# One row of the HGRN stage's table rewritten: gates as steps of their own, masked copies and a vector-matrix product placed elsewhere

## The chip, the core and the metric

The kernel runs on one core of a Trainium2 chip, in one launch. A core has five engines that run side by side, each through its own queue in order: PE (matmul; its weight loads are shown apart as PEld), DVE (elementwise), ACT (activation functions, copies), POOL (elementwise, no access to PSUM) and SP, which here only issues DMAs. Engines wait for each other through semaphores. The metric is device time in microseconds, over several runs; a profile is one further execution, whose own time and whose span (first to last instruction) are both given.

## The reference, cut to what matters

The program is two decoder blocks on 256 tokens of width 1024. The first has an HGRN2 mixer, a SwiGLU network, an attention layer and a second network; the second block has four small attention mixers and a convolutional network. All is fp32. The change lies in the HGRN2 mixer of the first layer and touches the conditioning vectors computed beside it:

```python
mod = c_act @ mod_w[layer] + mod_b[layer]                 # (1, 1024) @ (1024, 6144)
sh1, sc1, g1, sh2, sc2, g2 = jnp.split(mod, 6, axis=-1)
u = modulate(rms_norm(h, norm_mix[layer]), sh1, sc1)
q, z_f, v, g = jnp.split(u @ w_in, ...)                   # (256, 1024) @ (1024, 4096)
q = jax.nn.silu(q)
sig = jax.nn.sigmoid(z_f)
f = lbf + (1 - lbf) * sig                                 # the gate, per token and key channel
log_f = jnp.log(jnp.maximum(f, 1e-30))
k = (1 - lbf) * (1 - sig)
# per chunk of 64 tokens and head: attn[t, s] = sum_d q[t] * exp(cumsum difference) * k[s]
# o = attn @ v + (q * exp(b)) @ state;  state = exp(b_last) * state + (k * ...) @ v
o = o * lax.rsqrt(mean(o * o) + eps) * o_gain * silu(g)
h = h + g1 * (o @ w_out)
u = modulate(rms_norm(h, norm_ffn[layer]), sh2, sc2)      # into the SwiGLU network
```

## The kernel before, in words

Activations lie transposed in SBUF: 128 channels on the partitions, tokens along the free side; 256 tokens of two heads, a "pair", are one 128x512 tile. There are four pairs (0 to 3). A weight of 512 KB is a "unit". SP loads it into one of 7 raw buffers; ACT casts it to a high part (`w_hi`, line 193), DVE subtracts to get the low part (`w_lo`, line 195), and PE takes three products per tile (lines 258 to 260: high by high, high by low, low by high). `pump` (before each step of the program) issues loads as raw buffers come free and converts units at most two ahead of the one in use.

The HGRN stage begins with the products of f for pairs 0 and 1 and of q for all pairs (`lin_first`, line 809 in the new text, 806 in the old; the last quarter is `lf[3]`, three units). When the last quarter of f is done, `ev_f` takes the sigmoid on ACT and calls `gates_of` at once: for each head two DVE instructions (lines 748 and 749), and one more for the pair (line 750), five in all per pair; then `hg_t`, six short POOL multiplies (line 856) that give the products of f over 2, 4, ... 64 tokens, `dp`.

The rest of the stage is a list of short steps whose order is written by hand in the string `HG_ORDER`. The first letter is the kind, the first digit the pair:

- `f30` is the first half of a product of f for pair 3 (24 matmuls of 256 columns; `f20`, `f21`, `f31` alike), `v0` to `v7` are the eight units of v (12 matmuls of 512 columns), `w..` those of the output gate; `fa`, `fb`, `fc` are the gates of pairs 2 and 3 from their products, in three steps, the last with four ACT instructions and the DVE line 750.
- `s08` to `s00` are the scores of pair 0 at nine distances (PE: levels 8 to 3 are 16 matmuls of 32x32 tiles, line 896; each bank of PSUM, `pb_b`, of which there are three, holds two levels; 2, 1 and 0 are lines 915, 909, 902). Level 8 reads q, the others `qp` = q times f, made by `d0` (DVE line 847).
- `u06` to `u00` follow each level: a POOL multiply of k (lines 867, 873) and a DVE multiply of `qp` (lines 868, 874) by the products of f of that length. The scores of the next level need both.
- `c00`, `c01`, `c02` take a full score bank out of PSUM by masked copies into `cb` (DVE line 926, two per step; the third also copies on DVE and ACT, line 930). Only then is the bank free.
- `t2`, `t3` are `hg_t` for the later pairs; `pv`, `sq`, `st`, `r`, `n`, `m`, `o`, `ol` are output and norm of a pair, and `a0` to `a5` the output product with its residual.
- `y20` to `y27` are the eight units of the vector-matrix product for g1, on DVE: two instructions a step on raw weights into `ga` (line 516 first, then line 518). `y30`.. and `y40`.. (sh2 and sc2) are on PE: eight small matmul records a step (line 524). `q2` sums up, `z2`, `z3`, `z4` put the vectors in place.

Each engine runs its instructions in the order of this string, so what stands late on DVE delays whatever waits for DVE.

Of the kernel before, what the change touches and what calls it, by code (L numbers as in the profile page):

```python
# [11 lines left out]
F32R = mybir.dt.float32r  # L12
# [34 lines left out]
tr5 o0 y46 y47 pv4 tr6 o1 o2 z3 q4 pv5 pv6 tr7 o3 pv7 z4 o4 o5  # L47
"""
HG_ORDER = """
d0 d1 y20 f20 f21 s08 s18 s07 s17 u06 u16 y21 f30 fa2 c00 c10 s06 s16 u05 u15 fb2 y22 f31 s05 s15 c01 c11 u04  # L50
u14 fc2 y23 y30 v0 fa3 s04 s14 u03 u13 fb3 y31 v1 s03 s13 c02 c12 u02 u12 fc3 d2 y32 y24 v2 s28 s27 s02 s12 u01
u11 u26 t2 y33 v3 s01 s11 u00 u10 c20 s26 u25 d3 y34 v4 s00 s10 s38 s37 u36 s25 u24 t3 y35 y25 v5 pv0 sq0 c21
s24 u23 c30 s36 u35 y36 v6 st0 r0 s23 u22 s35 u34 y37 y26 v7 n0 pv1 sq1 c22 s22 u21 c31 s34 u33 z3 w00 st1 r1
s21 u20 s33 u32 y27 y40 w01 n1 s20 c32 s32 u31 y41 w10 wa0 s31 u30 pv2 sq2 wb0 y42 q2 w11 wc0 s30 st2 r2 m0 wa1
y43 w20 o0 wb1 ol0 pv3 sq3 n2 wc1 y44 z2 w21 m1 st3 r3 y45 w30 o1 ol1 wa2 n3 y46 w31 wb2 wc2 m2 y47 a0 wa3 o2
ol2 wb3 a1 wc3 m3 z4 a2 o3 ol3 a3 a4 a5
"""


# [72 lines left out]
def kernel(ctx: ExitStack, tc: tile.TileContext, x, c, mod_w, mod_b, norm_mix, norm_ffn,  # L132
# [19 lines left out]
    def slot(i, dt=F32, w=2048):  # L152
        return big.tile([P, w], dt, name=f"s{i}", tag=f"s{i}", bufs=1)
# [573 lines left out]
    T = {}  # L727
# [8 lines left out]
        T["v"] = [v[:, 0:D], v[:, D:2 * D]]  # L736

    steps.append(Step(start_hgrn))
    qf_evac = []
    def gates_of(sg, j):  # L740
        for m in range(2):
            h = 2 * j + m
            s_ = sg[:, 256 * m:256 * m + 256]
            if j > 1:
                SC.activation(T["f"][:, h], s_, AF.Identity, bias=lb[:, h:h + 1], scale=one_lb[:, h:h + 1])
                SC.activation(T["k"][:, h], s_, AF.Identity, bias=one_lb[:, h:h + 1], scale=cols[:, 24 + h:25 + h])
                continue
            DV.tensor_scalar(T["f"][:, h], s_, one_lb[:, h:h + 1], lb[:, h:h + 1], op0=OP.mult, op1=OP.add)
            DV.tensor_scalar(T["k"][:, h], s_, cols[:, 24 + h:25 + h], one_lb[:, h:h + 1], op0=OP.mult, op1=OP.add)
        DV.tensor_scalar(pair("f", j), pair("f", j), 1e-30, None, op0=OP.max)  # L750

    def pair(n, j):
        return T[n][:, 2 * j:2 * j + 2].rearrange("p k t -> p (k t)")

    def sig_a(t):
        DV.tensor_scalar(t, t, 2.0 ** 60, None, op0=OP.min)

    def sig_b(t):

        SC.activation(t, t, AF.Ln, bias=ones[:, 0:1], scale=1.0)  # L760
        SC.activation(t, t, AF.Exp, scale=-1.0)

    for j in range(2):
        def ev_f(p, j=j):
            sg = small(512, "sig", 2)
            SC.activation(sg, p, AF.Sigmoid)
            gates_of(sg, j)
            hg_t(j)
        qf_evac.append(ev_f)
    for j in range(4):  # L770
        def ev_q(p, j=j):
            SC.activation(T["q"][:, 2 * j:2 * j + 2].rearrange("p k t -> p (k t)"), p, AF.Silu)
        qf_evac.append(ev_q)
# [9 lines left out]
    for j in range(4):  # L783
        def ev_g(p, j=j):
            G[j] = small(512, "sq", 3)
            SC.activation(G[j], p, AF.Exp, scale=-1.0)
            DV.tensor_copy(pair("sg", j), p)
        for n, st in enumerate(lin_A(wa, 3072 + 256 * j, act("u0"), ev_g, acc_bank)):
            items[f"w{j}{n}"] = [st]
        items[f"wa{j}"] = [Step(lambda j=j: sig_a(G[j]))]  # L790
        items[f"wb{j}"] = [Step(lambda j=j: sig_b(G[j]))]
        items[f"wc{j}"] = [Step(lambda j=j: DV.tensor_mul(pair("sg", j), pair("sg", j), G[j]))]
    G = {}
    first = {}

    def lin_first(h, a, u):

        xhi, xlo = ubox["u0"]
        if h == 0 and a == 0:
            for n in range(2):  # L800
                first[n] = acc_bank()
            for w, x_, k in ((u.hi, xhi, 0), (u.hi, xhi, 1), (u.hi, xlo, 0), (u.hi, xlo, 1), (u.lo, xhi, 0), (u.lo, xhi, 1)):
                for n in range(2):
                    for m in range(2):
                        c0 = 256 * n + P * m
                        PE.matmul(first[n][:, 256 * m:256 * m + 256], lhsT=w[:, k, c0:c0 + P], rhs=x_[:, k],
                                  start=m == 0 and k == 0 and w is u.hi and x_ is xhi, stop=False, skip_group_check=True)
# [12 lines left out]
    lf = [[Step(lambda u, h=h, a=a: lin_first(h, a, u), [unit_A(wa, 256 * h, (1024, 0, 512)[a], 2, 512)], 2.6)  # L820
           for a in range(3)] for h in range(4)]
    for h in range(4):
        steps += [Step(lambda h=h: u0_part(h, LOOK if h == 3 else 1))] + [Step(start_w)] * (h == 3) + lf[h][:1]
        if h < 3:
            if h == 0:
                steps += xp[2:4]
            steps += gq[h + 1][:5] + lf[h][1:2] + gq[h + 1][5:] + lf[h][2:]
            if h == 2:
                steps += [Step(start_t)]
        else:  # L830
            steps += lf[h][1:]

    v_steps = []
    for j in range(2):
# [1006 lines left out]
    for i, it in enumerate(mixers):  # L1841
        kind, p = it
# [49 lines left out]
```

## Time and profile before

| | |
|---|---|
| time, median of 3 runs | 1148.94 us (1146.13 to 1149.74) |
| the profiled execution's own time | 1142.66 us |
| its span | 1140.9 us |
| PE busy, share of the span | 1098.1 us, 96% |
| DVE, ACT, POOL busy | 763.4, 573.4, 138.1 us |
| mean granted PE clock | 0.994 |

A busy PE is not PE at its peak, since matmuls overlap; what PE lost is read from its idle time and from the granted clock. The HGRN stage's hand-ordered list runs from about 68 us to about 197 us of the span. In the rows, `s` is one of the big slots (q, k, f, v lie there), `pb_acc` and `pb_b` are PSUM banks.

### The profile page before, as it was taken

What the parts mean: (1) busy time and instruction counts of PE and PEld (TensorE: products, weight loads), DVE (VectorE), ACT (ScalarE), POOL (GpSimd) and SP (SyncE); (2) the same over time, 40 slices, a digit from 0 to 9 for tenths busy, and PEclk for the clock granted to TensorE, in tenths of its full rate; (3) what the DMA queues carried; (4) which work ended last, traced back from release to release, by engine and by line L of the source; (5) the groups of instructions that cost most, each with busy time, mean ns of one, the idle gap of its engine ahead of it and who ended that gap; (6) DMA issues with size and microseconds to landing.
All of it is one profiled execution on the core that took longest, in us unless ns stands there. A gap on an engine that the chain in (4) does not pass through costs nothing.

```text
span 1140.9 us, 23598 instructions
## 1 busy us (share of the span) xinstructions
PE 1098.1 (96%) x9689; PEld 1014.4 (89%) x9689; DVE 763.4 (67%) x1237; ACT 573.4 (50%) x913; POOL 138.1 (12%) x201
## 2 busy tenths in 40 slices
PE   6988999999999999999999999999999999999997
PEld 4885789899999979888999999988888999999997
DVE  3586765787787688885564454667766766666666
ACT  3455464644444566555444444646555544554454
POOL 4044400000000001250000000013312100000000
PEclk9998999999999999999999999999999999999999
DMA  9976777798988777865766556773343656555651
GB/s 276 318 262 205 224 223 239 257 298 305 302 280 298 232 237 234 292 239 170 237 197 209 185 188 169 153 214 112 116 145 94 217 183 191 186 183 185 192 178 56
DMA packets 176125, 241.92 MB, mean 212 GB/s; under 512 B 18713, under 2 KB 142161, under 8 KB 176017
## 3 DMA queue, kind: packets, MB, share of 16 engines
q1 hardware_dynamic: 174928, 239.54, 66.4%
q8 instruction: 76, 1.25, 0.4%
q0 software_dynamic: 912, 0.81, 0.3%
q14 instruction: 33, 0.26, 0.1%
q10 hardware_dynamic: 176, 0.07, 0.0%
HBM read 239.33 MB, written 1.05 MB: 211 GB/s over the span
## 4 chain that ended last, share of the span: by engine, by line
PE 82%; DVE 6%; DMA 4%; ACT 4%; issue 2%; POOL 1%; SPq 0%; DVEq 0%; ACTq 0%; POOLq 0%
PE pb_b L258 14%; PE pb_b L260 14%; PE pb_b L259 14%; PE pb_acc L258 11%; PE pb_acc L260 10%; PE pb_acc L259 10%; DVE w_lo L195 2%; DMA w_raw<-in_a_w_in_dram 2%; ACT w_hi L193 2%; PE pb_b L463 1%; PE pb_b L1216 1%; DMA w_raw<-in_mod_w_dram 1%; DMA w_raw<-in_kv_w_dram 1%; PE pb_gv L524 1%; DVE nt L573 1%
## 5 line engine op out<-in xcount | busy, mean ns | idle before, releaser
L195 DVE TENSOR_TENSOR w_lo<-w_raw,w_hi 128x1024 fp32r<-128x1024 f32 (+1 forms) x335 | 409.3, 1246 | 172.7 <-ACT w_hi L193 172.0
L258 PE MATMUL pb_b<-s,w_hi 128*128 128x256 f32 x1488 | 419.4, 282 | 5.1 <-ACT s L1750 2.9
L260 PE MATMUL pb_b<-s,w_lo 128*128 128x256 f32 x1488 | 416.2, 280 | 1.6 <-DVE w_lo L195 1.5
L259 PE MATMUL pb_b<-s,w_hi 128*128 128x256 f32 x1488 | 417.3, 280 | 0.3
L193 ACT CAST w_hi<-w_raw 128x1024 fp32r<-128x1024 f32 (+1 forms) x336 | 342.1, 1043 | 79.3 <-DMA w_raw<-in_a_w_in_dram 19.2
L258 PEld LDWEIGHTS pb_b<-s,w_hi 128*128 128x128 f32 x1488 | 280.3, 188 | 12.7 <-issue 4.0
L260 PEld LDWEIGHTS pb_b<-s,w_lo 128*128 128x128 f32 x1488 | 280.3, 188 | 2.6 <-DVE w_lo L195 2.6
L259 PEld LDWEIGHTS pb_b<-s,w_hi 128*128 128x128 f32 x1488 | 280.3, 188 | 1.9 <-DVE s L585 0.7
L260 PE MATMUL pb_acc<-s,w_lo 128*128 128x256 f32 x656 | 183.4, 280 | 4.0 <-DVE w_lo L195 4.0
L258 PE MATMUL pb_acc<-s,w_hi 128*128 128x256 f32 x656 | 186.7, 285 | 0.6 <-ACT w_hi L193 0.6
L259 PE MATMUL pb_acc<-s,w_hi 128*128 128x256 f32 x656 | 183.1, 279 | 0.0
L258 PEld LDWEIGHTS pb_acc<-s,w_hi 128*128 128x128 f32 x656 | 123.3, 188 | 5.8 <-issue 3.5
L260 PEld LDWEIGHTS pb_acc<-s,w_lo 128*128 128x128 f32 x656 | 123.3, 188 | 4.8 <-DVE w_lo L195 4.8
L259 PEld LDWEIGHTS pb_acc<-s,w_hi 128*128 128x128 f32 x656 | 123.4, 188 | 0.2
L1209 POOL TENSOR_SCALAR att<-att,sm 128x128 f32<-128x128 f32 (+1 forms) x72 | 46.7, 668 | 619.4 <-DVE sm L1202 337.7
L1063 ACT CAST s<-sig 128x512 fp32r<-128x512 f32 x38 | 23.6, 621 | 115.9 <-DVE sig L1073 115.9
L258 PE MATMUL pb_acc<-w_hi,s 128*128 128x512 f32 x192 | 78.3, 408 | 1.7 <-ACT s L579 1.0
L259 PE MATMUL pb_acc<-w_lo,s 128*128 128x512 f32 x192 | 76.6, 399 | 0.8 <-DVE w_lo L195 0.8
L260 PE MATMUL pb_acc<-w_hi,s 128*128 128x512 f32 x192 | 76.5, 399 | 0.0
L1776 ACT ACTIVATE sig<-att,vb_t,vc_t 128x256 f32<-128x256 f32 x32 | 17.5, 595 | 75.4 <-DVE att L1771 75.4
L1069 ACT ACTIVATE sig<-pb_b 128x512 f32<-128x512 f32 x22 | 13.2, 598 | 77.8 <-PE pb_b L260 77.7
L1786 POOL TENSOR_TENSOR sig<-sig,rstd 128x512 f32<-128x512 f32 x16 | 22.7, 1420 | 237.2 <-ACT sig L1784 237.2
(373 smaller groups left out, 1255.7 us busy)
## 6 DMA issues: line engine op xcount, KB each, us to landing
w_raw<-in_mod_w_dram SPq DMA_DIRECT2D x96, 512.0 KB, 4.9
w_raw<-in_ffn_w_in_dram SPq DMA_DIRECT2D x88, 512.0 KB, 5.2
w_raw<-in_ffn_w_out_dram SPq DMA_DIRECT2D x44, 512.0 KB, 4.8
w_raw<-in_a_w_in_dram SPq DMA_DIRECT2D x32, 512.0 KB, 5.5
w_raw<-in_ffn_w_gate_dram SPq DMA_DIRECT2D x32, 512.0 KB, 3.8
w_raw<-in_ffn_w_up_dram SPq DMA_DIRECT2D x32, 512.0 KB, 5.3
w_raw<-in_ffn_w_down_dram SPq DMA_DIRECT2D x32, 512.0 KB, 3.6
w_raw<-in_kv_mod_w_dram SPq DMA_DIRECT2D x16, 512.0 KB, 5.8
```

The source lines that it names most:

```text
L193: SC.copy(hi, raw)
L195: DV.tensor_sub(lo, raw, hi.bitcast(F32))
L258: PE.matmul(o, lhsT=whi, rhs=xhi, start=start, stop=False, skip_group_check=True)
L259: PE.matmul(o, lhsT=whi, rhs=xlo, start=False, stop=False, skip_group_check=True)
L260: PE.matmul(o, lhsT=wlo, rhs=xhi, start=False, stop=stop, skip_group_check=True)
L463: PE.matmul(st[:, 0:256], lhsT=mean_d, rhs=sq[:, 256 * m:256 * m + 256], start=j == 0 and m == 0, stop=j == n - 1 and m == 1)
L524: PE.matmul(g[32 * j:32 * j + 32, 0:256], lhsT=by, rhs=r, start=start, stop=stop, tile_position=(0, 32 * j))
L1063: SC.copy(hi, hid)
L1069: SC.activation(sg, g, AF.Silu)
L1209: GP.tensor_scalar(t[:, i, cs], t[:, i, cs], r[:, 2 * b + i:2 * b + i + 1], 1.0, op0=OP.mult, op1=OP.mult)
L1776: SC.activation(zm, am, AF.Identity, bias=vcol("conv_b")[:, f:f + 1], scale=vc_t[:, 64 + f:65 + f])
L1786: GP.tensor_mul(zp, zp, rs_pair())
```

## The change

Four things, all in the HGRN stage:

1. The gates of pairs 0 and 1 are no longer computed inside the evacuation of f. `ev_f` keeps the sigmoid, and two new steps, `first_gates(0)` and `first_gates(1)`, stand between the units of `lf[3]`. Since `pump` runs before each step, a conversion of a coming unit falls before each.
2. In `HG_ORDER` the masked copies come directly after the scores and updates of their bank (`c00 c10` before `f30`, `c01 c11` after `u04 u14`, `c20` before `t2`, `c30 c21` before `t3`), and `d2` (`qp` of pair 2) moves from behind `c02 c12 u02 u12 fc3` to before them.
3. The vector-matrix products change places: `y4` (PE) is first, one unit between products, `y2` (DVE) starts at its old fourth part and runs to the end of the pairs' scores, and `y3` (PE) comes last. No unit is added or removed.
4. The split of the outputs (`ohi`, `olo`) lies in slots 3 and 4, which held q and k, instead of in eight tiles of the stage's pool.

```diff
 HG_ORDER = """
-d0 d1 y20 f20 f21 s08 s18 s07 s17 u06 u16 y21 f30 fa2 c00 c10 s06 s16 u05 u15 fb2 y22 f31 s05 s15 c01 c11 u04
+d0 d1 f20 f21 s08 s18 s07 s17 u06 u16 c00 c10 y40 f30 fa2 s06 s16 u05 u15 fb2 y41 f31 s05 s15 u04 u14 c01 c11
...
@@ gates
-    qf_evac = []
+    qf_evac, G = [], {}
...
             SC.activation(sg, p, AF.Sigmoid)
-            gates_of(sg, j)
-            hg_t(j)
+            G["f", j] = sg
         qf_evac.append(ev_f)
+
+    def first_gates(j):
+        gates_of(G["f", j], j)
+        hg_t(j)
+
...
-            steps += lf[h][1:]
+            for j in range(2):
+                steps += [Step(lambda j=j: first_gates(j))] + lf[h][1 + j:2 + j]
...
     def hg_o(p):
         o = T["f"][:, 2 * p:2 * p + 2].rearrange("p k t -> p (k t)")
-        hi, lo = ph(512, "ohi", 4, F32R), ph(512, "olo", 4, F32R)
+        if p == 0:
+            T["ohi"], T["olo"] = slot(3, F32R), slot(4, F32R)
+        hi, lo = (T[n][:, 512 * p:512 * p + 512] for n in ("ohi", "olo"))
```

First place, on DVE at the end of `lf[3]`: the five gate instructions of pair 0, then of pair 1 (`s_257` is f, `s_256` is k, `cols` the lower bounds), and the low parts of the next units.

```order
 L724 TENSOR_SCALAR cols<-cols 128x8
+L195 TENSOR_TENSOR w_lo<-w_raw,w_hi 128x1024
 L748 TENSOR_SCALAR s_257<-sig,cols 128x256
 L749 TENSOR_SCALAR s_256<-sig,cols 128x256
@@ -63,4 +64,5 @@
 L749 TENSOR_SCALAR s_256<-sig,cols 128x256
 L750 TENSOR_SCALAR s_257<-s_257 128x512
+L195 TENSOR_TENSOR w_lo<-w_raw,w_hi 128x1024
 L748 TENSOR_SCALAR s_257<-sig,cols 128x256
 L749 TENSOR_SCALAR s_256<-sig,cols 128x256
```

A low part now stands ahead of the gates of pair 0 and another between the pairs, where all three stood behind both.

Second place, on DVE from the first `qp` to the update of level 5, before: `ga` is the sum of `y2`, `cb` the masked copies' target.

```order
L847 TENSOR_TENSOR qp<-s_254,s_257 128x512 x2
L516 TENSOR_SCALAR ga<-w_raw,ca 128x512 x2
L195 TENSOR_TENSOR w_lo<-w_raw,w_hi 128x1024
L874 TENSOR_TENSOR qp<-qp,s_257 128x256 x2
L518 SCALAR_TENSOR_TENSOR ga<-w_raw,ca,ga 128x512 x2
L195 TENSOR_TENSOR w_lo<-w_raw,w_hi 128x1024
L756 TENSOR_SCALAR s_256<-s_256 128x512
L926 COPY_PREDICATED cb<-pairm,pb_b 128x128 x4
L874 TENSOR_TENSOR qp<-qp,dp 128x128x2 x2
```

And the same stretch now (lines are shifted by 4):

```order
L851 TENSOR_TENSOR qp<-s_254,s_257 128x512 x2
L195 TENSOR_TENSOR w_lo<-w_raw,w_hi 128x1024
L878 TENSOR_TENSOR qp<-qp,s_257 128x256 x2
L930 COPY_PREDICATED cb<-pairm,pb_b 128x128 x4
L195 TENSOR_TENSOR w_lo<-w_raw,w_hi 128x1024
L756 TENSOR_SCALAR s_256<-s_256 128x512
L878 TENSOR_TENSOR qp<-qp,dp 128x128x2 x2
```

The four masked copies stand directly behind the updates; the `ga` instructions are gone from here.

Third place, on DVE around the single `qp` of pair 2 (`d2`), before:

```order
L926 COPY_PREDICATED cb<-pairm,pb_b 128x128 x2
L930 COPY ab_964<-cb 32x4x32 x2
L926 COPY_PREDICATED cb<-pairm,pb_b 128x128 x2
L930 COPY ab_986<-cb 32x4x32 x2
L874 TENSOR_TENSOR qp<-qp,dp 128x16x16 x2
L750 TENSOR_SCALAR s_257<-s_257 128x512
L847 TENSOR_TENSOR qp<-s_254,s_257 128x512
L518 SCALAR_TENSOR_TENSOR ga<-w_raw,ca,ga 128x512 x2
```

And now:

```order
L756 TENSOR_SCALAR s_256<-s_256 128x512
L878 TENSOR_TENSOR qp<-qp,dp 128x32x8 x2
L851 TENSOR_TENSOR qp<-s_254,s_257 128x512
L195 TENSOR_TENSOR w_lo<-w_raw,w_hi 128x1024
L878 TENSOR_TENSOR qp<-qp,dp 128x16x16 x2
L930 COPY_PREDICATED cb<-pairm,pb_b 128x128 x2
L934 COPY ab_958<-cb 32x4x32 x2
L930 COPY_PREDICATED cb<-pairm,pb_b 128x128 x2
```

`qp` of pair 2 now stands ahead of the last masked copies and of the gate instruction of pair 3 (line 750), which it followed.

## Rows read from the trace of the kernel before

**Rows 1.** Page, busy time of each engine over the span.

```profile
PE 1098.1 (96%) x9689; PEld 1014.4 (89%) x9689; DVE 763.4 (67%) x1237; ACT 573.4 (50%) x913; POOL 138.1 (12%) x201
```

**Rows 2.** Busy time by stretch: length; PE, PEld, DVE, ACT, POOL (instructions); clock; DMA.

```profile
60.00:112.00 52.00, 43.20 (x740) 36.54 (x740) 39.53 (x82) 28.55 (x46) 23.88 (x36) 0.93 0.72 234
112.00:150.00 38.00, 35.98 (x587) 28.64 (x585) 28.22 (x48) 17.71 (x32) 13.93 (x22) 1.00 0.70 218
...
100.00:104.00 4.00, 0.91 (x35) 0.43 (x33) 2.64 (x10) 3.33 (x9) 0.20 (x1) 0.92 0.68 239
104.00:108.00 4.00, 3.47 (x75) 2.47 (x76) 3.94 (x7) 2.01 (x6) 2.24 (x1) 0.50 0.26 54
108.00:112.00 4.00, 4.00 (x23) 3.03 (x22) 0.00 (x0) 1.18 (x3) 3.61 (x9) 0.73 0.89 316
```

**Rows 3.** PE's waits, 60 to 200 us: for whom, us in total, times, longest.

```profile
PE pb_b L498 <- ACT ab L918: 1.0, 1, 1.0
PE pb_b L896 <- POOL s L867: 0.9, 1, 0.9
```

**Rows 4.** PE in order of time, 67.5 to 84.5: start, length, instruction [idle before].

```profile
70.82 0.39 PE L260 MATMUL pb_acc<-s,w_lo 128*128 128x256 f32 x1 [2.08 <-DVE w_lo L195]
...
77.61 0.38 PE L258 MATMUL pb_acc<-s,w_hi 128*128 128x256 f32 x1
...
83.52 0.46 PE L896 MATMUL pb_b<-qp,s 128*32 128x32 f32 x32 [2.45 <-DVE cb L926]
```

**Rows 5.** DVE in order of time, 62 to 104 us.

```profile
65.74 0.41 DVE L748 TENSOR_SCALAR s<-sig,cols 128x256 f32<-128x256 f32 x1 [0.90 <-ACT sig L766]
...
67.37 0.41 DVE L748 TENSOR_SCALAR s<-sig,cols 128x256 f32<-128x256 f32 x1
...
69.51 2.41 DVE L195 TENSOR_TENSOR w_lo<-w_raw,w_hi 128x1024 fp32r<-128x1024 f32 x2
...
73.56 1.59 DVE L847 TENSOR_TENSOR qp<-s,s 128x512 f32<-128x512 f32 x2
...
78.80 2.02 DVE L518 SCALAR_TENSOR_TENSOR ga<-w_raw,ca,ga 128x512 f32<-128x512 f32 x2
...
103.45 0.43 DVE L750 TENSOR_SCALAR s<-s 128x512 f32<-128x512 f32 x1 [1.20 <-ACT s L745]
```

**Rows 6.** ACT in order of time, 62 to 82 us: the casts of two units.

```profile
66.07 1.05 ACT L193 CAST w_hi<-w_raw 128x1024 fp32r<-128x1024 f32 x1
...
69.41 1.05 ACT L193 CAST w_hi<-w_raw 128x1024 fp32r<-128x1024 f32 x1
```

**Rows 7.** POOL in order of time, 62 to 145 us.

```profile
71.94 0.61 POOL L856 TENSOR_TENSOR dp<-s 128x256 f32<-128x256 f32 x1
72.63 3.37 POOL L856 TENSOR_TENSOR dp<-dp 128x128 f32<-128x128 f32 x5
...
77.50 2.11 POOL L873 TENSOR_TENSOR s<-s,s 128x256 f32<-128x256 f32 x2 [0.28 <-PE pb_b L896]
...
105.76 3.25 POOL L873 TENSOR_TENSOR s<-s,dp 128x256 f32<-128x256 f32 x2 [4.98 <-PE pb_b L915]
...
110.45 1.67 POOL L856 TENSOR_TENSOR dp<-dp 128x128 f32<-128x128 f32 x5
```

**Rows 8.** PE in order of time, 97 to 112 us, around the scores of pair 2.

```profile
97.46 0.50 PE L258 MATMUL pb_acc<-w_hi,s 128*128 128x512 f32 x1
...
100.45 0.46 PE L896 MATMUL pb_b<-s,s 128*32 128x32 f32 x32
104.53 0.66 PE L896 MATMUL pb_b<-qp,s 128*32 128x32 f32 x32 [3.62 <-DVE qp L847]
...
106.81 0.80 PE L258 MATMUL pb_acc<-w_hi,s 128*128 128x512 f32 x1
...
111.30 1.15 PE L909 MATMUL pb_b<-qp,s 128*64 128x64 f32 x16
```

**Rows 9.** The chain that ended last, in order of time: one step of `y4` on PE.

```profile
169.99 0.57 PE pb_gv L524 x8
```

More of the change, by code (lines that the diff above doesn't have):

```diff
@@ L49 @@
 HG_ORDER = """
-d0 d1 y20 f20 f21 s08 s18 s07 s17 u06 u16 y21 f30 fa2 c00 c10 s06 s16 u05 u15 fb2 y22 f31 s05 s15 c01 c11 u04
[L51 to L56, printed above, removed]
+d0 d1 f20 f21 s08 s18 s07 s17 u06 u16 c00 c10 y40 f30 fa2 s06 s16 u05 u15 fb2 y41 f31 s05 s15 u04 u14 c01 c11
+fc2 y42 v0 fa3 s04 s14 u03 u13 fb3 d2 y43 v1 s03 s13 u02 u12 c02 c12 fc3 y20 y44 v2 s28 s27 s02 s12 u01 u11 u26
+c20 t2 y45 v3 s01 s11 u00 u10 s26 u25 d3 y46 v4 s00 s10 s38 s37 u36 s25 u24 c30 c21 t3 y47 y21 v5 pv0 sq0 s24
+u23 s36 u35 z4 v6 st0 r0 s23 u22 s35 u34 c22 c31 y22 v7 n0 pv1 sq1 s22 u21 s34 u33 y23 y30 w00 st1 r1 s21 u20
+s33 u32 c32 y24 w01 n1 s20 s32 u31 y25 y31 w10 wa0 s31 u30 pv2 sq2 wb0 y26 w11 wc0 s30 st2 r2 m0 wa1 y27 y32 w20
+o0 wb1 ol0 pv3 sq3 n2 wc1 y33 w21 m1 st3 r3 q2 w30 o1 ol1 wa2 n3 y34 z2 w31 wb2 wc2 m2 y35 a0 wa3 o2 ol2 wb3 y36
+a1 wc3 m3 y37 a2 o3 ol3 a3 a4 a5 z3
 """
@@ L792 @@
         items[f"wc{j}"] = [Step(lambda j=j: DV.tensor_mul(pair("sg", j), pair("sg", j), G[j]))]
-    G = {}
     first = {}
```

## The prediction

> **What bounds the kernel now.** I read the page first: PE is busy for 1098.1 of 1140.9 us [rows 1], so whatever the change brings is time in which PE stood or ran slowly in the HGRN stage. The table by stretch says how much that is [rows 2]. From 60 to 112 us PE is busy for 43.20 of 52.00, so 8.8 us are idle; from 112 to 150 another 2.0. The stretches of 4 us add the clock: PE did only 0.91 us of work from 100 to 104, the granted clock was 0.92 there, then 0.50, then 0.73. A stretch with mean clock x was at half speed (1.2 instead of 2.4 GHz) for a share of 2(1 - x), so 0.64 + 4.0 + 2.16 = 6.8 us ran at half speed, and a stretch of PE work at half speed loses half of its length, 3.4 us at most. All that this change can give back is thus 8.8 + 2.0 + 3.4 = 14.2 us.
>
> Then I followed PE in order of time and looked for gaps. Three make up most of the idle time, and each names what stood ahead on DVE. **A**: 2.08 us at 70.82, a product of f that waits for its low part [rows 4]; its cast was done at 66.07 + 1.05 = 67.12 [rows 6], but DVE ran ten gate instructions from 65.74 to 69.5, and only then the low part [rows 5]. **B**: 2.45 us at 83.52, level 6 of pair 1, which waits for its bank: the masked copies stand behind two `ga` instructions of 2.02 us, a low part and line 756. **C**: 3.62 us at 104.53, level 7 of pair 2, which waits for `qp` of pair 2; that ran at 103.79, behind the gate instruction of pair 3 at 103.45, which waited for ACT [rows 5, 8]. The view of waits has two small ones behind these, 0.9 and 1.0 us [rows 3].
>
> **The change part by part.** I walk along PE and set the new time of each landmark beside the old. A step of `y4` costs PE 0.57 us [rows 9]. It replaces `y3` steps of the same kind, so only how many of them were done before a landmark matters.
>
> *Gates as steps.* The low part of f20 comes ahead of all gates: cast done at 67.12, low part 1.2 (half of 2.41), ready at 68.4; PE asked for it at 70.82 - 2.08 = 68.74. A goes. The second: cast done at 69.41 + 1.05 = 70.46, low part at 71.7, and a wait of about 0.3 us. But the gates do not vanish from DVE's queue. Five take 1.7 us (65.74 to 67.4) where nothing runs beside them, and the second five took 2.2 (67.37 to 69.58) beside POOL. So DVE does: gates of pair 0 to 70.1, low part to 71.7, gates of pair 1 to 73.9, low part to 75.1, two `qp` of 0.8 (half of 1.59) to 75.9 and 76.7. Scores of level 7 need `qp`: pair 1's last until about 77.0, then one step of `y4`, and the product f30 starts at 77.6, where it started at 77.61. So what A gives comes back as a wait ahead of level 7; PE has only one step of `y4` more behind it. Gain 0.6. From both sides: with no interference between DVE and POOL the gates of pair 1 take 1.7, and the gain is 0.5 more; if all the rest of DVE's work there (5.7 us) goes as slowly as those five did, 2.2 for 1.7, it takes 1.7 more, and PE loses 1.1.
>
> *POOL behind it.* The products of pair 1 (`hg_t`) start 2 us later, at 73.9 instead of 71.94, and took 0.6 and 3.4, so 4.1 [rows 7]; to 78.0. POOL's four memsets after them took until 77.50 - 0.28 = 77.2, some 1.3 us; so to 79.3. The updates of k, 1.05 each (half of 2.11), end at 80.3 and 81.4. Level 6 of pair 0 starts at 80.6 as before (83.52 - 2.45 - 0.46), level 6 of pair 1 at 81.5 instead of 83.52, since the masked copies now stand directly behind the updates of `qp`, without the `ga` pair and the low part. B shrinks from 2.45 to about 0.5. f31 then starts at 82.5 (with a second step of `y4`) instead of 83.91: gain 1.4 on the clock, and 2 steps (1.14) done in advance. The same six POOL instructions took 0.61 + 1.67 = 2.3 later [rows 7]; with that, B is gone whole and the gain 0.5 higher. The other end: POOL as slow as the two updates at 105.76 (3.25 instead of 2.11) gives 1.0 less.
>
> *f31 to v2.* From f31 to the end of v2 took 100.45 - 83.91 = 16.5 us and has the same work; some 0.4 of idle time in it goes. It ends at 98.7.
>
> *`d2` moved.* `qp` of pair 2 now comes some ten us before level 7 wants it, right behind `fb3`. C goes whole. Levels 8 and 7, two levels 2 and a step of `y4` took 0.46, and 106.81 - 104.53 = 2.3 at a falling clock [rows 8]; I take 2.0 for all of it at full speed; v3 starts at 100.7 instead of 106.81, a gain of 6.1. By then six steps of `y4` are done and before there were four of `y3`: two steps, 1.14.
>
> *The clock.* With no gap of 4 us ahead of it, v3 runs at 2.4 GHz. It took 111.30 - 106.81 = 4.49; v2, the same twelve matmuls, took 100.45 - 97.46 = 3.0 [rows 8]. It ends at 103.7. The next step is level 1 of pair 0, whose update of `qp` is now late: it stands on DVE behind the gate of pair 3, which waits for ACT, and behind `ga` of `y20`. I put level 1 at 104.3, where it was 111.30: gain 7.0, and with the two steps 8.1. Between 103.7 and 104.9 all is possible; at its worst the clock falls again there, which takes back up to the 3.4 us above.
>
> *What comes to stand later.* Of the eight `ga` pairs of `y2` four stood ahead of 100 us and now stand behind, so DVE has 4 x 2.02 = 8 us more to do there. It is busy for 28.22 of 38 us from 112 to 150 [rows 2], so they find room; what it costs if they don't is the third rival. Half of the waits of 0.9 and 1.0 goes, as their copies and updates come earlier: +0.9. Slots for `ohi` and `olo` I cost at nothing: k and q are no longer read by then, and nothing else claims the slots; the copies are the same.
>
> Sum: 8.1 + 0.9 = 9.0. The profiled execution took 1142.66, so 1133.7; it lies 6.28 below the median of the timed runs, so 1148.94 - 9.0 = **1140** for the median. Bounds: at the low end 9.0 - 1.7 (DVE) - 1.0 (POOL) - 2.6 (three quarters of the clock's loss stays) = 3.7; at the high end 12.5, as 14.2 less the waits that the walk still has ahead of levels 7, 6 and 1.
>
> One rule speaks against the walk. DVE runs from 70 to 77 us without a pause now, two-input instructions mostly, with POOL beside it. In the trace two POOL updates took 3.25 us at 105.76, and 2.11 at 77.50 [rows 7]; DVE was busy for 3.94 of the 4 us from 104 to 108 [rows 2]. The Trainium skill, "SBUF — State Buffer", section "Who interferes with whom", says that a VectorE instruction with two inputs in SBUF and a GpSimd instruction that reads SBUF exclude each other, the first to issue keeping the other out for its whole length. The trace agrees as far as these rows go. By the rule the products of pair 1 would stand whole instructions long behind low parts and `qp`; without it they would take 2.3.
>
> **Rivals.** *POOL becomes the bound.* If DVE's unbroken run keeps the products of pair 1 out until its end at about 76.7, they end at 79.0 (2.3 us alone), with memsets and updates at 82.4 to 83.5; level 6 of pair 1 is where it was (-2.0). The update before level 1 meets DVE in the same way once more (3.25 for 2.11, -1.1), and DVE held up in turn makes level 7 later (-0.9, half of the 1.7 above). Gain 5, time 1144. For it: the five gates that took 2.2 beside POOL. Against it: 4.1 was measured with three low parts and two `qp` beside them already. 0.14. *The clock falls all the same*, from the waits before levels 7, 6 and 1 following each other: gain 9 less 2.5 (between v3's own 1.5 and 3.4), time 1142.4. Against it: the waits of 2.08 and 2.45 before did not do it by themselves. 0.14. *Stalls change places.* The gate instruction of pair 3 stays where ACT lets it, at 103.45; behind it `ga` 2.0, a low part 1.2, an update 1.0: level 1 starts at 108.1, gain 3.2 + 1.1, and less 2.5 if the clock falls in that wait: 1.8, time 1147. For it: ACT has as many casts ahead of it as before. Against: `fc3` now stands behind shorter PE work. 0.12. *Slower:* `ga` pairs stand in front of a low part in seven places behind 104 us, where before it was four; 7 x 2.02 = 14 us. If each low part were late by its pair and PE waited for all of it, the sum would be 9 - 14 = -5, time 1154; from 9 us uncovered on it is slower than before. Against it: from 112 to 150, with such pairs in the program, all of PE's idle time is 2.0, and 1.9 of it is for POOL and ACT [rows 2, 3]. 0.08.
>
> **How the numbers follow.** The forecast (gain 6 to 12.5) has 0.52. The first two rivals are faster too: 0.80. 0.3%, 3.4 us, is what a measurement can tell here; stalls that only change places lie within it: 0.12; slower 0.08. The range goes from 1148.94 - 14.2 = 1134.7 to 1148.94 - 3.7 = 1145.2, widened by the 1.8 us over which the timed runs spread to either side: 1133 to 1147.
>
> **What would show it.** The idle times of A and C are gone, B's is under 1 us, the clock is 1.00 from 96 to 112. New, small waits stand before level 7 of pairs 0 and 1 (for `qp` of line 847), level 6 of pair 1 (for POOL) and level 1 of pair 0. v3 starts near 100.7 and takes 3.0. All that follows the pairs' scores is some 9 us earlier and else the same. Wrong would be: a wait over 2 us ahead of level 7 or 6, a clock below 1 from 100 to 112, or PE idle time on a low part after 112, which was nearly zero.

## The result, and the profile after

The changed kernel takes 1138.09 us (median of 6, 1134.69 to 1140.26), against 1148.38 for the kernel before in the same rounds. The ratio is 0.9915, 95% interval 0.9898 to 0.9931, so the gain is 9.8 us (7.9 to 11.7), 0.85%, near the forecast 9.0 (the two medians themselves differ by 10.3). Its profiled execution took 1137.38 us with a span of 1135.6.

Line numbers of the functions are 4 higher than before. The first view is the busy time by stretch (columns as in rows 2), over the same stretches of the span; this execution began the stage 1.75 us later than the one of before.

```profile
60.00:112.00 52.00, 47.35 (x822) 39.10 (x821) 42.22 (x86) 31.96 (x51) 26.55 (x40) 1.00 0.70 235
112.00:150.00 38.00, 37.98 (x572) 31.48 (x571) 29.88 (x53) 20.50 (x38) 16.03 (x18) 1.00 0.75 241
...
100.00:104.00 4.00, 4.00 (x115) 2.90 (x114) 1.89 (x7) 3.33 (x9) 2.52 (x5) 1.00 0.52 193
104.00:108.00 4.00, 2.19 (x22) 1.64 (x20) 3.97 (x8) 3.93 (x9) 3.26 (x7) 1.00 0.36 99
108.00:112.00 4.00, 3.88 (x55) 2.84 (x54) 4.00 (x7) 1.53 (x3) 2.34 (x4) 1.00 1.05 392
```

PE's idle time from 60 to 112 us falls from 8.8 to 4.65, the 2.0 from 112 to 150 are gone, and the clock is 1.00 throughout (0.50 and 0.73 in two rows of before [rows 2]). PE's waits from 60 to 200 us of the changed kernel (for whom, total, times, longest):

```profile
PE pb_b L913 <- POOL dp L860: 1.8, 1, 1.8
PE pb_b L900 <- POOL s L877: 1.3, 1, 1.3
PE pb_b L258 <- ACT s L579: 1.2, 1, 1.2
PE pb_b L900 <- DVE qp L851: 0.7, 2, 0.4
PE pb_acc L260 <- DVE w_lo L195: 0.3, 1, 0.3
```

None of A, B and C is left under its old name. In their place stand waits at the places that the prediction's walk along PE named: 0.3 on the second low part, 0.4 twice ahead of level 7, 1.3 for POOL ahead of level 6 of pair 1, and 1.8 ahead of level 1 of pair 0 (the view names POOL there; e7 and e10 below show that it was DVE and ACT). The 1.2 for ACT lies behind the stage, at 198.62; the kernel before has it too, at 205.99. In order of time on PE (start, length, instruction, idle before):

```profile
73.59 0.39 PE L260 MATMUL pb_acc<-s,w_lo 128*128 128x256 f32 x1 [0.31 <-DVE w_lo L195]
77.51 0.46 PE L900 MATMUL pb_b<-qp,s 128*32 128x32 f32 x32 [0.40 <-DVE qp L851]
78.32 0.46 PE L900 MATMUL pb_b<-qp,s 128*32 128x32 f32 x32 [0.35 <-DVE qp L851]
84.16 0.46 PE L900 MATMUL pb_b<-qp,s 128*32 128x32 f32 x32 [1.32 <-POOL s L877]
...
102.15 0.50 PE L258 MATMUL pb_acc<-w_hi,s 128*128 128x512 f32 x1
...
107.03 1.12 PE L913 MATMUL pb_b<-qp,s 128*64 128x64 f32 x16 [1.81 <-POOL dp L860]
```

The two profiles don't start alike: the first sigmoid of f, ahead of which nothing was changed, ended its wait at 65.10 before and at 66.85 here. So every start below is counted from that sigmoid. This is the start of the matmul with which the named piece begins, in the profiled execution of each kernel; "next" is a matmul of the network behind the stage, the same one in all.

| kernel | f31 | v3 | v4 | w00 | next | ratio to before (95%) |
|---|---|---|---|---|---|---|
| before | 18.8 | 41.7 | 49.1 | 71.7 | 164.4 | 1 |
| after | 18.2 | 35.3 | 42.3 | 62.9 | 155.4 | 0.9915 (0.9898 to 0.9931) |
| e1_gates_only | 20.0 | 45.0 | 52.5 | 75.1 | 167.8 | 1.0017 (1.0000 to 1.0034) |
| e2_gates_back | 18.1 | 35.3 | 42.3 | 62.8 | 155.2 | 0.9909 (0.9891 to 0.9928) |
| e3_d2_only | 19.0 | 39.6 | 47.4 | 70.8 | 163.6 | 0.9976 (0.9963 to 0.9989) |
| e4_d2_back | 18.2 | 38.9 | 45.3 | 65.9 | 158.3 | 0.9929 (0.9910 to 0.9948) |
| e5_split_gates | 16.4 | 33.5 | 40.5 | 61.0 | 153.4 | 0.9880 (0.9861 to 0.9900) |
| e7_y20_late | 18.2 | 35.3 | 42.0 | 62.6 | 155.1 | 0.9900 (0.9883 to 0.9917) |
| e8_y_back | 17.2 | 36.2 | 44.7 | 66.7 | 159.2 | 0.9934 (0.9916 to 0.9952) |
| e9_copies_back | 17.4 | 34.5 | 41.0 | 65.2 | 158.6 | 0.9928 (0.9909 to 0.9947) |
| e10_fc3_late | 18.2 | 35.3 | 41.0 | 61.5 | 153.9 | 0.9878 (0.9856 to 0.9901) |
| e11_best | 16.1 | 33.2 | 38.9 | 59.4 | 151.9 | 0.9872 (0.9853 to 0.9891) |
| e12_best_memsets | 16.2 | 33.3 | 38.9 | 59.5 | 152.0 | 0.9855 (0.9833 to 0.9877) |

The landmarks are of one execution each, the ratios of all timed runs, so the two need not agree. The stage gave 164.4 - 155.4 = 9.0 us. The spans differ by only 5.3, since this execution began the stage 1.75 us later and lost another 2 us behind it, most of it at about 855 us, where the code is unchanged: both kernels have a wait of 2.9 us for ACT there, and behind it the clock was lower in this execution than in that of before. Busy time by stretch there, of the changed kernel:

```profile
854.00:858.00 4.00, 4.00 (x23) 4.00 (x22) 3.14 (x7) 2.83 (x6) 2.66 (x4) 0.57 0.00 0
```

and of the kernel before, some 6 us later:

```profile
860.00:864.00 4.00, 4.00 (x32) 4.00 (x31) 3.41 (x9) 2.53 (x6) 3.33 (x4) 0.86 0.00 0
```

### The profile page after: what moved, and what is told of

It reads as the page before. It is cut to its first block, busy times and chain, and to the rows that moved or that the text cites. A ratio compares the mean times of both kernels' runs of the same rounds, so it can differ in the third digit from the quotient of the medians.

```text
span 1135.6 us, 23604 instructions
## 1 busy us (share of the span) xinstructions
PE 1098.3 (97%) x9689; PEld 1014.6 (89%) x9689; DVE 763.1 (67%) x1237; ACT 572.9 (50%) x913; POOL 141.7 (12%) x201
## 4 chain that ended last, share of the span: by engine, by line
PE 84%; DVE 5%; ACT 4%; DMA 3%; POOL 2%; issue 1%; SPq 0%; DVEq 0%; ACTq 0%; POOLq 0%
PE pb_b L258 15%; PE pb_b L260 15%; PE pb_b L259 14%; PE pb_acc L258 11%; PE pb_acc L260 10%; PE pb_acc L259 10%; DMA w_raw<-in_a_w_in_dram 2%; ACT w_hi L193 2%; DVE w_lo L195 2%; PE pb_b L463 1%; POOL dp L860 1%; PE pb_gv L524 1%; PE pb_b L1222 1%; DVE nt L573 1%; DMA w_raw<-in_mod_w_dram 1%
## 5 line engine op out<-in xcount | busy, mean ns | idle before, releaser
L258 PE MATMUL pb_acc<-s,w_hi 128*128 128x256 f32 x720 | 205.2, 285 | 1.8 <-ACT w_hi L193 1.7
L260 PE MATMUL pb_acc<-s,w_lo 128*128 128x256 f32 x720 | 201.5, 280 | 2.6 <-DVE w_lo L195 2.6
L259 PE MATMUL pb_acc<-s,w_hi 128*128 128x256 f32 x720 | 201.0, 279 | 0.1
L258 PEld LDWEIGHTS pb_acc<-s,w_hi 128*128 128x128 f32 x720 | 135.3, 188 | 9.2 <-issue 5.0
L260 PEld LDWEIGHTS pb_acc<-s,w_lo 128*128 128x128 f32 x720 | 135.3, 188 | 3.4 <-DVE w_lo L195 3.4
L259 PEld LDWEIGHTS pb_acc<-s,w_hi 128*128 128x128 f32 x720 | 135.4, 188 | 0.5 <-DVE s L585 0.3
L1075 ACT ACTIVATE sig<-pb_b 128x512 f32<-128x512 f32 x22 | 13.2, 598 | 75.1 <-PE pb_b L260 75.1
```

The costliest lines, as they stand in the source:

```text
L258: PE.matmul(o, lhsT=whi, rhs=xhi, start=start, stop=False, skip_group_check=True)
L259: PE.matmul(o, lhsT=whi, rhs=xlo, start=False, stop=False, skip_group_check=True)
L260: PE.matmul(o, lhsT=wlo, rhs=xhi, start=False, stop=stop, skip_group_check=True)
L1075: SC.activation(sg, g, AF.Silu)
```

## The experiments

**One part alone, or one part undone.**

e1_gates_only, on the kernel before:

```diff
-            gates_of(sg, j)
-            hg_t(j)
+            G["f", j] = sg
...
-            steps += lf[h][1:]
+            for j in range(2):
+                steps += [Step(lambda j=j: first_gates(j))] + lf[h][1 + j:2 + j]
```

> The kernel before, with the gates of pairs 0 and 1 as steps between the products, and nothing else changed. Times in the profile are counted from the first sigmoid of f (before: f30 starts at 12.5, v3 at 41.7, level 1 of pair 0 at 46.2). Theory 'walk': the wait on the low part of 2.1 us falls to 0.3, but DVE ends its work ahead of level 7 just as late, so waits for qp stand there and f30 starts between 12.3 and 13.3; the waits of 2.5 (masked copies) and 3.6 (qp of pair 2) stay; gain in time between -1 and +1 us. Rival 'the wait itself': the 2.1 us go through to the end, f30 starts at 10.5, gain 2 us. Rival 'POOL': the products of pair 1 end 2 us later and take the place of the masked copies, level 6 of pair 1 later by 1 us or more, loss 1 to 2 us.

Measured: 2 us slower (0 to 3.9). f30 starts at 11.86, earlier than the walk's 12.3 to 13.3. The wait on the low part fell to 0.3, as all theories had it, but the wait for the masked copies grew from 2.5 to 3.4 (not for POOL's sake: on DVE the copies run at 84.89, behind `ga`, a low part and line 756 without a pause). Waits of PE in e1:

```profile
PE pb_b L900 <- DVE qp L851: 4.5, 3, 3.7
PE pb_b L900 <- DVE cb L930: 3.4, 1, 3.4
```

and its stretches from 80 us:

```profile
80.00:84.00 4.00, 1.66 (x43) 1.35 (x41) 4.00 (x5) 0.65 (x1) 4.00 (x7) 1.00 0.82 248
84.00:88.00 4.00, 2.34 (x40) 2.31 (x41) 3.93 (x10) 1.35 (x2) 1.61 (x2) 0.52 0.74 258
88.00:92.00 4.00, 4.00 (x86) 3.87 (x88) 0.61 (x1) 0.51 (x2) 0.00 (x0) 0.63 0.45 139
```

Behind B the clock is down to half for most of these two stretches (0.52, 0.63), which it wasn't in the profiled execution of before. A shorter wait at one place bought a longer one at the next; that was missed by the walk, and the POOL rival has the size, but not the cause. How much of the clock's fall is due to the edit is not shown: e3 below has such a fall with B unchanged.

e2_gates_back, on the changed kernel: `gates_of` and `hg_t` inside `ev_f` again, `steps += lf[h][1:]`.

> The changed kernel with its gates of pairs 0 and 1 put back into the evacuation of f; all else as changed (there f30 starts 12.3 us behind the first sigmoid, f31 at 18.2, v3 at 35.3, level 1 of pair 0 at 40.2). Theory 'walk': the wait on the low part comes back with 2.1 us, the two waits for qp of 0.4 and the one of 1.3 for POOL go, as POOL's products start earlier; f31 starts between 17.2 and 18.7, v3 between 34.5 and 36; time within 1.5 us of the changed kernel, so 8 to 11 us under before. Rival 'the wait itself': the steps are worth their 2.1 us, f31 at 20, gain 7.5 us.

Measured: 0.9909, beside 0.9915 for the changed kernel, and the same landmarks from f31 on (18.14 and 18.18). The waits of e2 up to there:

```profile
PE pb_acc L260 <- DVE w_lo L195: 2.1, 1, 2.1
...
PE pb_b L900 <- issue: 0.8, 1, 0.8
```

2.1 + 0.8 stand for 0.3 + 0.7 + 1.3. The 0.8 stands at 84.66, at the end of level 6 and ahead of `y41`; the profile names no releaser for it and the walk did not have it, so its cause stays open. With it in, the walk's landmarks are right, and the gates as two steps are worth nothing here.

e3_d2_only, on the kernel before:

```diff
-u13 fb3 y31 v1 ... fc3 d2 y32
+u13 fb3 d2 y31 v1 ... fc3 y32
```

> The kernel before with the qp of pair 2 moved from behind the last gates of pair 3 to before them (ahead of the second unit of v), and nothing else changed. Theory 'walk': the wait of 3.6 us goes, the clock stays at 1.00 and the fourth unit of v takes 3.0 instead of 4.5; level 1 of pair 0 then waits for DVE (gate of pair 3, ga, low part, update) until some 41.5 us behind the first sigmoid, where it was at 46.2; gain 4 to 5.5 us in all. Rival 'clock by itself': the clock falls also without the wait, v3 takes 4.5 as before, gain at most 3.6. Rival 'the stall changes place': level 1 waits until 44 or later, gain 2 or less.

Measured: 2.7 us faster (1.3 to 4.2), less than the walk said. C is gone, v3 takes 3.0, but level 1 starts only 44.75 us behind the sigmoid, and level 2 has a wait of its own, since copies stand ahead of its update. PE in e3:

```profile
104.53 0.71 PE L915 MATMUL pb_b<-qp,s 128*32 128x32 f32 x29 [0.98 <-DVE qp L874]
...
110.81 1.12 PE L909 MATMUL pb_b<-qp,s 128*64 128x64 f32 x16 [2.08 <-POOL dp L856]
```

That is the third rival, "the stall changes place", in part. DVE shows why: the update that level 1 needs runs at 110.16, behind the gate of pair 3, `ga` and a low part.

```profile
105.92 0.69 DVE L750 TENSOR_SCALAR s<-s 128x512 f32<-128x512 f32 x1 [1.20 <-ACT s L745]
106.53 2.37 DVE L518 SCALAR_TENSOR_TENSOR ga<-w_raw,ca,ga 128x512 f32<-128x512 f32 x2
108.82 1.42 DVE L195 TENSOR_TENSOR w_lo<-w_raw,w_hi 128x1024 fp32r<-128x1024 f32 x1
110.16 0.89 DVE L874 TENSOR_TENSOR qp<-qp,dp 128x256 f32<-128x256 f32 x2
```

e3 shows one thing more. Its program is the one of before up to there, and B is the same wait, 2.46 us; yet behind it the clock fell:

```profile
84.00:88.00 4.00, 3.52 (x46) 3.48 (x47) 3.33 (x7) 1.18 (x2) 0.92 (x1) 0.57 0.54 199
```

In the profiled execution of before that stretch has 1.00. So B costs more than its 2.5 us in some executions and not in others. That fits the profiled execution of before being 6 us under its median, and a timed gain slightly above the stage's 9.0; how often it falls there the runs don't tell. Behind the 2.08 us ahead of level 1 the clock of e3 fell again (0.98 and 0.59 in the stretches from 108 and 112 us). By 2(1 - x) each fall is 3.4 us at half speed, so up to 1.7 us lost, and e3's 0.8 us at "next" holds both; the timed 2.7 is the better price of `d2` alone.

e4_d2_back, on the changed kernel: `d2` behind `fc3` again.

> The changed kernel with the qp of pair 2 put back behind the last gates of pair 3. Theory 'walk': level 7 of pair 2 waits 3.5 to 4 us again, the granted clock falls to 0.5 behind it, v3 takes 4.5; level 1 of pair 0 comes 4 to 6 us later than in the changed kernel (its own wait of 1.8 is swallowed); gain over before 4 to 6 us. Rival 'no clock loss': the wait is there, the clock stays at 1.00 since the work ahead of it is denser now; loss against the changed kernel 2 to 2.5, gain 7.5 us.

Measured: level 7 of pair 2 waits 3.44 us, v4 comes 3.1 us later than in the changed kernel, and the time is 8.1 us (6.0 to 10.3) under before. The clock:

```profile
100.00:104.00 4.00, 1.11 (x36) 0.58 (x34) 1.88 (x8) 3.33 (x9) 0.21 (x1) 1.00 0.56 190
104.00:108.00 4.00, 3.46 (x77) 2.58 (x78) 3.94 (x9) 2.02 (x6) 2.59 (x2) 0.76 0.36 105
108.00:112.00 4.00, 4.00 (x61) 3.12 (x62) 0.00 (x0) 2.07 (x4) 3.61 (x10) 0.81 0.79 260
```

It falls, against the rival, but only to 0.76 and 0.81: 2(1 - x) of 4 us is 1.9 + 1.5 us at half speed, 1.7 us lost, where before lost up to 3.4. The loss is 3.1 instead of 4 to 6: the mechanism holds, its price was set too high, and the gain over before (8.1) lies nearer to the rival's 7.5 than to the walk's 4 to 6.

e8_y_back, on the changed kernel: the three products where they stood before.

```diff
-d0 d1 f20 f21 s08 s18 s07 s17 u06 u16 c00 c10 y40 f30 fa2 s06 s16 u05 u15 fb2 y41 f31
+d0 d1 y20 f20 f21 s08 s18 s07 s17 u06 u16 c00 c10 y21 f30 fa2 s06 s16 u05 u15 fb2 y22 f31
...
```

> The changed kernel with the three vector-matrix products at the places they have before (y2 first, on DVE between the early products); gates, copies and qp of pair 2 as changed. Theory 'walk': ga lies ahead of the qp update and of low parts again, f31 (with no y step on PE ahead of it; 18.2 with two in the changed kernel) starts between 17.5 and 19.5, level 1 of pair 0 waits 2 to 3.5 us instead of 1.8 for the update behind ga; in all 1 to 3 us slower than the changed kernel, gain over before 6.5 to 8.5. Rival 'regrouping is the change': without it the copies are late all the same, the wait for them stays above 2 us and the clock falls behind it; gain 3 us or less.

Measured: 0.9934, some 2 us slower than the changed kernel in time and 3.8 at "next". f31 starts at 17.2 with no step of `y4` on PE ahead of it (18.2 - 1.14 = 17.1 in the changed kernel, so the same); waits of 0.3 to 0.8 stand at most levels, and 2.2 at level 1. Behind that one the clock fell, which the walk did not have:

```profile
108.00:112.00 4.00, 2.58 (x52) 2.37 (x56) 3.97 (x8) 3.22 (x7) 2.47 (x4) 0.68 0.70 230
112.00:116.00 4.00, 4.00 (x24) 2.78 (x17) 3.06 (x5) 0.67 (x1) 0.97 (x3) 0.89 0.60 172
```

By the prediction's 2(1 - x) that is 3.4 us at half speed, so up to 1.7 of the 3.8. The rival is out: the waits for copies are 0.3 and 0.4 without the regrouping.

e9_copies_back, on the changed kernel:

```diff
-u06 u16 c00 c10 y40 f30 fa2 s06 ... u04 u14 c01 c11 fc2
+u06 u16 y40 f30 fa2 c00 c10 s06 ... c01 c11 u04 u14 fc2
...
-s33 u32 c32 y24 w01 n1 s20 s32
+s33 u32 y24 w01 n1 s20 c32 s32
```

> The changed kernel with the masked copies at the places they have before (behind the half product and gates step, or ahead of the qp updates); the rest as changed. Theory 'walk': level 6 of pair 1 waits for POOL anyway, and its copies are now late by about as much (wait 1.3 to 2 us); the third copies ahead of the updates of level 2 bring a wait of about 1 us; the clock stays at 1.00; 0.5 to 1.5 us slower than the changed kernel. Rival 'copies are the change': the wait of 2.5 us for the bank comes back, with a fall of the clock behind it: 3 us or more slower.

Measured: 3.2 us slower at "next", 1.5 in time (0.9928 to 0.9915, within the intervals). But the loss lies elsewhere than either theory put it. Early, the old places are better: f31 at 17.4 instead of 18.2. The loss is at the later pairs, 2.46 us for a copy at 130.21 alone, with the clock at 1.00 behind it (lines are 3 lower than in the changed kernel):

```profile
130.21 0.43 PE L897 MATMUL pb_b<-qp,s 128*32 128x32 f32 x29 [2.46 <-DVE cb L927]
```

Why early copies cost something is seen on DVE and POOL. The copies and the updates of k after level 7 in the changed kernel:

```profile
80.93 1.25 DVE L930 COPY_PREDICATED cb<-pairm,pb_b 128x128 f32<-128x128 int32 x4 [0.70 <-POOL cb L892]
81.48 2.63 POOL L877 TENSOR_TENSOR s<-s,s 128x256 f32<-128x256 f32 x2
```

and in e9:

```profile
80.50 1.83 POOL L874 TENSOR_TENSOR s<-s,s 128x256 f32<-128x256 f32 x2
```

In the changed kernel the copies wait 0.70 us for POOL's memset of `cb` (line 892), and a low part runs on DVE right behind them, inside those 2.63 us; in e9 the low part goes ahead of the copies and had ended at 80.4. The Trainium skill, "SBUF — State Buffer", section "Who interferes with whom", has it that VectorE instructions with two SBUF inputs and GpSimd instructions that read SBUF keep each other out; these two rows agree. The runs of e11 and e12 below differ in the same way, 1.94 us at 78.61 with the low part ahead and 2.82 at 78.81 beside it. With the place of the copies most of the changed kernel's wait of 1.32 for POOL goes; two of 0.3 are left.

**What is left in the changed kernel.**

e5_split_gates, on the changed kernel:

```diff
             G["f", j] = sg
+            if j == 0:
+                first_gates(0)
...
-            for j in range(2):
-                steps += [Step(lambda j=j: first_gates(j))] + lf[h][1 + j:2 + j]
+            steps += [Step(lambda: first_gates(1))] + lf[h][1:]
```

> The changed kernel with the gates of pair 0 back in the evacuation of f, ahead of the first low part, and those of pair 1 as a step behind it. Times from the first sigmoid of f (changed kernel: f30 12.3, f31 18.2, v3 35.3). Theory 'two queues': the step as made puts the low part first and both gates late, so DVE (level 7) and POOL (level 6 of pair 1) are late by what PE no longer waits; split, the low part is ready at 3.5, where PE wants it at 3.6, POOL starts two us earlier, and the waits of 0.3, 0.4, 0.4 and 1.3 us all go: f31 between 15.8 and 16.6, 2 us under the changed kernel, gain over before 11 to 12.5 us. Rival 'DVE and POOL exclude each other': the products of pair 0 then lie beside the low parts and both take longer; f31 between 17.5 and 18.5, nothing gained.

Measured: f31 at 16.4, 1.8 us under the changed kernel, and 1.8 it stays; time 0.9880, 13.8 us under before (11.5 to 16.0). Both waits ahead of level 7 go, and POOL's falls from 1.32 to 0.76, where the theory had it gone; on PE in e5:

```profile
80.33 0.46 PE L901 MATMUL pb_b<-qp,s 128*32 128x32 f32 x32 [0.76 <-POOL s L878]
```

e7_y20_late, on the changed kernel:

```diff
-fc3 y20 y44 v2 s28 s27 s02 s12 u01 u11 u26 c20 t2 y45
+fc3 y44 v2 s28 s27 s02 s12 u01 u11 u26 c20 t2 y20 y45
```

> The changed kernel with the first ga step of y2 moved from behind the last gates of pair 3 to behind the products of pair 2 (t2), so that it no longer stands ahead of the update that level 1 of pair 0 needs. The trace of the changed kernel names POOL (the products of pair 2) for the wait of 1.8 us there. Theory 'DVE': the true releaser is the DVE update behind ga; the wait falls to 0.5 us or less, v4 starts at 40.7 to 41.2 behind the first sigmoid instead of 42.3. Rival 'POOL': the wait stays between 1.5 and 2 us. In time 1 to 1.5 us under the changed kernel by the one, the same by the other.

Measured: the wait is still 1.48, v4 at 42.0. Not the forecast, and yet not POOL. DVE in e7, around the update that level 1 needs (105.66; PE starts at 106.32):

```profile
102.94 0.67 DVE L750 TENSOR_SCALAR s<-s 128x512 f32<-128x512 f32 x1 [2.00 <-ACT s L745]
104.52 1.23 DVE L195 TENSOR_TENSOR w_lo<-w_raw,w_hi 128x1024 fp32r<-128x1024 f32 x1 [0.91 <-ACT w_hi L193]
105.66 0.89 DVE L878 TENSOR_TENSOR qp<-qp,dp 128x256 f32<-128x256 f32 x2
```

`ga` is gone, and the low part now waits 0.91 us for its cast. On ACT the cast stands behind the gates of pair 3:

```profile
101.18 0.60 ACT L745 ACTIVATE s<-s,cols 128x256 f32<-128x256 f32 x1
101.81 0.60 ACT L746 ACTIVATE s<-s,cols 128x256 f32<-128x256 f32 x1
102.32 0.59 ACT L745 ACTIVATE s<-s,cols 128x256 f32<-128x256 f32 x1
102.94 0.60 ACT L746 ACTIVATE s<-s,cols 128x256 f32<-128x256 f32 x1
103.45 1.03 ACT L193 CAST w_hi<-w_raw 128x1024 fp32r<-128x1024 f32 x1
```

e10_fc3_late, on the changed kernel, the same with `fc3` moved as well: `... u26 c20 t2 fc3 y20 y45`.

> The changed kernel with the last gates of pair 3 (four ACT instructions and one on DVE) and the first ga step both moved behind the products of pair 2. Moving ga alone left 1.5 us of the wait before level 1 of pair 0: the low part ahead of the update then waited for its cast, which stood behind the four ACT instructions. Theory 'ACT': with these behind, cast, low part and update come 2 us earlier and the wait falls to 0.3 us or less; v4 starts 40.2 to 40.9 us behind the first sigmoid (changed kernel 42.3, ga alone late 42.0), and nothing else moves; 1.5 to 2 us under the changed kernel. Rival 'POOL', which the trace names: the wait stays at 1.5. Rival 'later gates': qp of pair 3 is late by as much, and its scores wait 1 us or more.

Measured: level 1 waits no more, v4 at 41.0, 1.3 us under the changed kernel (a wait of 0.4 for copies comes up behind it); time 0.9878. ACT it was, and not POOL: level 1 starts at 103.11 on PE, while POOL's products of pair 2, which the trace of the changed kernel named, still run:

```profile
102.60 0.80 POOL L860 TENSOR_TENSOR dp<-s 128x256 f32<-128x256 f32 x1
103.47 2.06 POOL L860 TENSOR_TENSOR dp<-dp 128x128 f32<-128x128 f32 x5
```

No score waits for the later gates.

e11_best: the edits of e5 and e10 together, and `c00 c10` at the place of e9.

> Three edits together on the changed kernel: the gates of pair 0 back in the evacuation and those of pair 1 as a step (worth 1.8 us by itself), the last gates of pair 3 and the first ga step behind the products of pair 2, and the first masked copies back behind the half product (worth 0.8 us at f31, where the copies stand beside POOL's updates). Theory: the three waits are independent and add up: f31 between 15.5 and 16.4 behind the first sigmoid, v4 at 38 to 39.2 (changed kernel 42.3), 3.2 to 4.5 us under the changed kernel. Rival: early gains are taken up at the next wait; no more than 2 us under it.

Measured: f31 at 16.1, v4 at 38.9, "next" 3.5 us under the changed kernel and 12.5 under before; the gains of e5 and e10 add up, while the copies' 0.8 at f31 is worth only 0.3 on top of e5 (16.1 to 16.4). In time 0.9872 (0.9853 to 0.9891). All that PE waits for from 60 to 200 us:

```profile
PE pb_b L258 <- ACT s L579: 1.2, 1, 1.2
PE pb_b L901 <- DVE cb L931: 0.4, 1, 0.4
PE pb_b L901 <- issue: 0.2, 1, 0.2
PE pb_acc L260 <- DVE w_lo L195: 0.2, 1, 0.2
```

e12_best_memsets: `ab` and `cb` of pairs 0 and 1 set to zero at the start of `first_gates`.

> The kernel with the three edits, and besides the four memsets of pairs 0 and 1 ahead of POOL's products instead of behind them. Theory 'POOL': the updates of k start 1.3 us earlier, the wait of level 6 of pair 1 (0.3 to 0.8 us) goes, f31 at 15.2 to 15.7. Rival: the updates then wait for the scores of level 7 on PE, and what is left is 0.2 us or less; the same time as without.

Measured: f31 at 16.2, all landmarks as in e11. That is the rival's result, but not for its reason: the updates of k start 0.5 us earlier than in e11, counted from the sigmoid, take 2.82 instead of 1.94 beside a low part, and level 6 of pair 1 then waits 0.49 for copies. Its ratio is 0.9855, with an interval that overlaps e11's widely. Both are the fastest kernels here at "next", 14.7 and 16.7 us under before in time; in time they can't be told apart, nor from e5 and e10.

## Why the prediction was right, step by step

The sum of 9.0 came out, and most of its steps do; two sizes that were off to one side were met by three off to the other.

*A gives nothing.* Right. The walk put f30 at the same time as before, with one step of `y4` done; it was 0.2 us earlier. e2 shows the steps to be worth nothing in the whole change.

*B.* Its own cause went as said, but the size was wrong: 0.5 us forecast, 1.32 measured, f31 18.2 instead of 17.4 behind the sigmoid. The walk's sign "B's is under 1 us" thus failed. It had POOL's products of pair 1 at 4.1 us and the two updates of k at 2.1; they took 4.9 and 2.63:

```profile
75.38 1.53 POOL L860 TENSOR_TENSOR dp<-s 128x256 f32<-128x256 f32 x1
76.99 3.30 POOL L860 TENSOR_TENSOR dp<-dp 128x128 f32<-128x128 f32 x5
```

They started 0.3 us earlier than the walk had them, so level 6 of pair 1 came 0.9 later. This is a mild form of the POOL rival, which put 2.0 us there and added two more effects (1.1 and 0.9) to come to a gain of 5.

*f31 to v2.* Forecast gain 0.4, measured 1.1 (18.81 to 32.36 before, 18.18 to 30.64 now). The walk saw no price in `ga` between scores here. e8, with the vector-matrix products and so `ga` back, has 4.65 and 4.77 us from v0 to v1 and v1 to v2, and the changed kernel 4.15 twice.

*C and the clock.* Right: v3 at 35.3 (forecast 35.6), and 3.0 us long. At "next" it is worth 0.8 us when it goes alone (e3) and 2.9 when it goes last (e4), but e3's profiled execution lost up to 3.4 us to the clock. In time it is 2.7 alone and 1.6 last, within the intervals; that its worth depends on its company is not shown.

*Level 1.* Forecast 39.2 behind the sigmoid, measured 40.2. The place was right, the cause incomplete: `ga` is 0.3 us of it, and the rest is the cast on ACT behind the last gates (e7, e10). (`y20` stands where `y24`, the fifth unit of `y2`, stood before.)

*The rest.* 0.9 forecast, as half of the two small waits [rows 3]; both are gone whole. At level 1 the gain was 46.2 - 40.2 = 6.0, with two steps of `y4` 7.1; at "next" it is 9.0, so 1.9 came behind level 1.

So the terms that were off were the length of POOL's products and updates beside DVE, and what stood ahead of level 1; they cost 0.8 us, and 1.3 from v3 (0.3 early) to level 1 (1.0 late). Back came 0.7 between f31 and v2, 0.3 in the scores ahead of v3 (1.7 us long instead of 2.0), and 1.0 from the small waits behind. That these cancel, and that the sum is right to 0.1 us at "next", is luck; the single steps are right to about 1 us.

Undone one by one in the changed kernel, at "next": the gates cost nothing, `qp` of pair 2 2.9 us, the regrouped products 3.8, the copies 3.2, in sum 9.9 for the 9.0 of the whole. These are single executions; by the timed ratios the same are worth -0.7, 1.6, 2.2 and 1.5 us, each by itself within the intervals. Alone, two were tried on the kernel before: the gates -2.0 us in time, `d2` 2.7. The regrouped products and the copies were not tried alone, so how far the parts need each other is not shown. What e1 and e3 do show is that where a wait goes, PE can run into a longer or a new one on the same DVE queue (3.4 at B in e1, 2.1 at level 1 in e3).

The fourth part, the slots for `ohi` and `olo`, was not undone by itself. It acts between w00 and "next", and that stretch took 92.7 us before and 92.5 now, with one step of PE fewer in it (0.57); no gain of its own is to be seen, as the prediction had it.

## What to carry to other kernels

Price a removed wait by walking to the next thing that PE will ask for, on every queue that was moved, and not by the wait's length; try parts of a rewritten order both alone and left out, and read their worth from the timed runs too, since one profiled execution can hold a fall of the clock that another lacks. Where several engines had to be done, the releaser that a profile names is the one that came last by its records: follow the operand that the waiting instruction reads. When two queues (DVE, POOL) hang on the same early work, split it so that each gets its first piece early, as in e5.

## What was not expected of the hardware

The same wait of PE, 2.45 and 2.46 us at the same instruction of the same program, was followed by a granted clock of 1.00 in one execution and 0.57 in another; behind waits of 3.4 to 3.7 us it fell each time (before, e1, e4). It fell behind 2.08 in e3 and 2.19 in e8, and stayed at 1.00 behind the 2.08 of A and the 2.46 in e9. A removed wait of this size is thus worth a varying amount. The timed runs vary in the same sense: of the 23 of the kernel before beside e1 to e4, the five with a mean granted clock of 0.987 took 1149.6 to 1150.9 us, and the six with 0.994 or more 1144.1 to 1147.3.
